# Max-pool, upsample and subtract: the first tile loaded and stored in two pieces of two rows in place of pieces of one, one and two

## The chip, the cores and the metric

The kernel runs on one core of one Trainium2 chip. The metric is the device time of one execution in microseconds, and a kernel's time is the median of several runs.

## The reference

The input x is float32 of shape 8 x 64 x 256 x 256. Every 8 x 8 window of an image is replaced by its maximum, the maxima are repeated back to the full size, and that is subtracted from x:

```python
x_r = x.reshape(B, C, oH, 8, oW, 8)
pooled = x_r.max(axis=(3, 5))
upsampled = np.repeat(np.repeat(pooled, 8, axis=2), 8, axis=3)
return x - upsampled
```

Input and output are 134.22 MB each; every byte is read once and written once.

## The kernel before

Eight image rows (one row of windows) are one "row" of the kernel: 2048 floats, 8 KB, with 32 windows in it. There are 16,384 such rows. A tile gives each of the 128 partitions 4 consecutive rows, 32 KB per partition and 4 MB in all, so there are 32 tiles, numbered 0 to 31. A part of R rows of a tile is R x 8 KB per partition; the profile shows R = 1 as 128x2048 and R = 2 as 128x4096.

The tiles live in SBUF in a ring of 6 slots (`ring`); the window maxima stand in `tops`. Tile i has slot (i - 1) modulo 6, so tile 0 shares slot 5 with tile 6.

Three engines share the work, and semaphores order them:

- SyncE (SP) issues the loads, L110, in order of the tiles. Tile 0 is loaded in pieces, one per entry of `HEAD`, each with a semaphore of its own (`first`); every other tile is loaded in one transfer. From tile 6 on a load first waits until the stores of the tile that had the slot before have landed (`stored`).
- TensorE computes nothing. It waits for the loads' semaphores in order (L117 for the pieces of tile 0, L120 for the others) and adds one to the count `filled` for each.
- VectorE takes one from `filled` (L75), reduces the windows of the part with one max (L81), and subtracts the maxima from the ring in place, one instruction per row (L93). It does that for each piece of tile 0, then in a loop over 5 rounds of 6 slots for tiles 1 to 30, and then for tile 31, which is loaded whole but worked on in the three pieces of `TAIL`, 2, 1 and 1 rows. After the last subtract of a part it adds one to `ready`.
- ScalarE (ACT) computes nothing either. It waits for the count `ready` and issues the store of that part (L129), in the pieces of `HEAD` for tile 0, whole for tiles 1 to 30, in the pieces of `TAIL` for tile 31. At the end it waits for the stores that no later load has waited for.

All loads go through SP's DMA queue, all stores through ACT's, and both queues feed the same 16 DMA engines.

Of the kernel before, what the change touches and what calls it, by code (L numbers as in the profile page):

```python
# [1 line left out]

# [4 lines left out]

F32 = mybir.dt.float32
ROW = 2048


HEAD = [1, 1, 2]
SIZE = 4
ROUNDS = 5
TAIL = [2, 1, 1]
SLOTS = 6


@with_exitstack
def kernel(  # L20
    ctx: ExitStack,
    tc: tile.TileContext,
    x: bass.AP,
    out: bass.AP,
):
    nc = tc.nc
    P = nc.NUM_PARTITIONS
    B, C, H, W = x.shape
    pH = pW = 8
    oW = W // pW  # L30

    x_rows = x.rearrange("b c (oh ph) w -> (b c oh) (ph w)", ph=pH)
    out_rows = out.rearrange("b c (oh ph) w -> (b c oh) (ph w)", ph=pH)
    sizes = [sum(HEAD)] + [SIZE] * (ROUNDS * SLOTS) + [sum(TAIL)]
    assert sum(sizes) * P == x_rows.shape[0] and max(sizes) == SIZE
    starts = [P * sum(sizes[:i]) for i in range(len(sizes))]
    last = len(sizes) - 1

    data = ctx.enter_context(tc.tile_pool(name="data", bufs=1))
    ring = data.tile([P, SLOTS * SIZE * ROW], F32, name="ring")  # L40
    tops = data.tile([P, SLOTS * SIZE * oW], F32, name="tops")
    first = [tc.alloc_semaphore(f"first{i}") for i in range(len(HEAD))]
    loaded = [tc.alloc_semaphore(f"loaded{i}") for i in range(SLOTS)]
    stored = [tc.alloc_semaphore(f"stored{i}") for i in range(SLOTS)]
    final = tc.alloc_semaphore("final")
    filled = tc.alloc_semaphore("filled")
    reduced = tc.alloc_semaphore("reduced")
    ready = tc.alloc_semaphore("ready")

    def slot_of(i):  # L50

        return (i - 1) % SLOTS

    def dram(rows, i):

        n = sizes[i]
        return rows[starts[i] : starts[i] + P * n].rearrange("(p r) d -> p (r d)", r=n)

    def sbuf(i, lo, R):
        at = (slot_of(i) * SIZE + lo) * ROW  # L60
        return ring[:, at : at + R * ROW]

    def top(i, lo, R):
        at = (slot_of(i) * SIZE + lo) * oW
        return tops[:, at : at + R * oW]

    def cuts(parts):
        lo = 0
        for R in parts:
            yield lo, R  # L70
            lo += R

    def take(sem, n):

        nc.vector.wait_ge(sem, n).then_inc(sem, -n)  # L75

    def pool_and_subtract(part, top, R):

        wins = part.rearrange("p (r ph ow pw) -> p r ph ow pw", r=R, ph=pH, ow=oW)
        maxs = top.rearrange("p (r ow) -> p r ow", r=R)  # L80
        nc.vector.tensor_reduce(  # L81
            out=maxs if R > 1 else maxs[:, 0],
            in_=(
                wins.rearrange("p r ph ow pw -> p r ow ph pw")
                if R > 1
                else wins[:, 0].rearrange("p ph ow pw -> p ow ph pw")
            ),
            axis=mybir.AxisListType.XY,
            op=mybir.AluOpType.max,
        ).then_inc(reduced, 1)  # L90
        take(reduced, 1)
        for r in range(R):
            sub = nc.vector.tensor_tensor(  # L93
                out=wins[:, r],
                in0=wins[:, r],
                in1=maxs[:, r].unsqueeze(1).unsqueeze(3).to_broadcast([P, pH, oW, pW]),
                op=mybir.AluOpType.subtract,
            )
        sub.then_inc(ready, 1)

    with tc.tile_critical(no_gpsimd_drain=True):

        landed = [0] * SLOTS
        for i in range(len(sizes)):
            slot = slot_of(i)
            if landed[slot]:
                nc.sync.wait_ge(stored[slot], 16 * landed[slot])
            for k, (lo, R) in enumerate(cuts(HEAD if i == 0 else [sizes[i]])):
                part = slice(lo * ROW, (lo + R) * ROW)
                nc.sync.dma_start(out=sbuf(i, lo, R), in_=dram(x_rows, i)[:, part]).then_inc(  # L110
                    first[k] if i == 0 else loaded[slot], 16
                )
                landed[slot] += 1


        for k in range(len(HEAD)):
            nc.tensor.wait_ge(first[k], 16).then_inc(filled, 1)  # L117
        for i in range(1, len(sizes)):
            turn = (i - 1) // SLOTS + 1
            nc.tensor.wait_ge(loaded[slot_of(i)], 16 * turn).then_inc(filled, 1)  # L120


        done = n_final = 0
        for i in range(len(sizes)):
            for lo, R in cuts(HEAD if i == 0 else TAIL if i == last else [SIZE]):
                part = slice(lo * ROW, (lo + R) * ROW)
                done += 1
                nc.scalar.wait_ge(ready, done)
                nc.scalar.dma_start(out=dram(out_rows, i)[:, part], in_=sbuf(i, lo, R)).then_inc(  # L129
                    stored[slot_of(i)] if i + SLOTS <= last else final, 16  # L130
                )
                n_final += i + SLOTS > last
        nc.scalar.wait_ge(final, 16 * n_final)


        for lo, R in cuts(HEAD):
            take(filled, 1)
            pool_and_subtract(sbuf(0, lo, R), top(0, lo, R), R)
        with nc.vector.Fori(0, ROUNDS):
            with nc.vector.Fori(0, SLOTS) as slot:  # L140
                take(filled, 1)
                pool_and_subtract(
                    ring[:, bass.ds(slot * (SIZE * ROW), SIZE * ROW)],
                    tops[:, bass.ds(slot * (SIZE * oW), SIZE * oW)],
                    SIZE,
                )
        take(filled, 1)
        for lo, R in cuts(TAIL):
            pool_and_subtract(sbuf(last, lo, R), top(last, lo, R), R)


# [1 line left out]
_INS = ['x']  # L153
_OUTS = [((8, 64, 256, 256), 'float32')]


# [23 lines left out]
```

## Time and profile before

| what | before |
|---|---|
| runs | 642.45, 643.52, 644.19 us; median 643.52 |
| profiled execution | 644.19 us, of which the span from the first to the last instruction is 642.4 |
| VectorE busy | 562.8 us, 88% of the span |
| VectorE idle before L81, for the count at L75 | 61.4 us in 27 waits |
| DMA | 268.44 MB, 418 GB/s over the span |
| loads of 4 MB, from issue to landing | 57.2 us (median of 31) |
| stores of 4 MB, from issue to landing | 44.8 us (median of 30) |
| max of one row, two rows, four rows | 2.28, 4.42, 8.69 us |
| subtract of one row | 2.29 us |

Engine names in the profile: DVE is VectorE, ACT is ScalarE, SP is SyncE, POOL is GpSimd; a q behind a name is the engine's instruction queue (SPq, ACTq, DVEq), which is where DMAs are issued and semaphores waited for. In the timeline a line has the start, the time taken (for a DMA line the stretch over which its issues lie), the engine, the line of the kernel, the operation, and in square brackets how long the engine idled before it and what ended that. In the table of windows the columns are the stretch, its length, VectorE's and GpSimd's busy time, the granted clock of TensorE, the share of the time in which the 16 DMA engines were busy, and what they moved in GB/s. The page's row of digits is the same share in 40 slices of 16 us. The trace also has a record of every DMA packet: its queue, its size, its start and its duration.

### The profile page before, as it was taken

The page shows a single profiled execution, that of the slowest core. Times are in us where ns is not written, and L with a number is a line of the kernel's source. Part 1 is how long each engine was busy: PE and PEld are TensorE (multiplying, and loading weights), DVE is VectorE, ACT ScalarE, POOL GpSimd, SP SyncE. Part 2 cuts the span into 40 slices and gives each one's busy share as a digit, 9 for nine tenths or more (in the row PEclk, how much of TensorE's full clock was granted, in tenths as well). Part 3 has the DMA queues.
Part 4 walks back from the last instruction along what each step waited for, and adds up shares of the span by engine and source line. Part 5 has one row for each costly group of instructions (what it writes and reads, how often), then busy time and mean ns, then how long its engine had stood idle before and what let it go on. Part 6 is the DMA issues. An engine that isn't in the chain of part 4 may idle for free. (4 is left out here: it accounts for less than half of the span.)

```text
span 642.4 us, 619 instructions
## 1 busy us (share of the span) xinstructions
DVE 562.8 (88%) x164; POOL 0.2 (0%) x4
## 2 busy tenths in 40 slices
DVE  6999999998889888889888998889988899888991
POOL 0000000000000000000000000000000000000000
DMA  9999999999999999999999999999999999999994
GB/s 367 441 416 441 424 422 433 431 437 422 420 424 437 424 416 431 414 433 424 416 422 420 428 428 414 426 422 426 424 420 424 426 420 426 424 424 412 428 418 203
DMA packets 10080, 268.44 MB, mean 418 GB/s; under 512 B 1120, under 2 KB 1120, under 8 KB 1120
## 3 DMA queue, kind: packets, MB, share of 16 engines
q1 hardware_dynamic: 4896, 134.22, 50.1%
q10 hardware_dynamic: 5184, 134.22, 48.5%
HBM read 134.22 MB, written 134.22 MB: 418 GB/s over the span
## 5 line engine op out<-in xcount | busy, mean ns | idle before, releaser
L81 DVE TENSOR_REDUCE tops<-ring (+2 forms) x36 | 278.5, 7736 | 61.4 <-DVEq L75 61.4
L93 DVE TENSOR_TENSOR ring<-ring,tops (+1 forms) x128 | 285.1, 2286 | 5.3 <-DVEq L75 0.2
L164 POOL MEMSET const-uint8-127<- 128x1 uint8 x1 | 0.1, 102 | 0.0
L164 POOL MEMSET const-bfloat16-1.0<- 128x1 bf16 x1 | 0.1, 101 | 0.0
L164 POOL MEMSET const-float32-0.0<- 128x1 f32 x1 | 0.1, 98 | 0.2 <-issue 0.2
L164 POOL MEMSET const-float32-1.0<- 128x1 f32 x1 | 0.1, 98 | 0.0
## 6 DMA issues: line engine op xcount, KB each, us to landing
ring<-in_x_dram SPq DMA_DIRECT2D x31, 4096.0 KB, 57.2
out_dram<-ring ACTq DMA_DIRECT2D x30, 4096.0 KB, 44.8
out_dram<-ring ACTq DMA_DIRECT2D x4, 1024.0 KB, 13.9
out_dram<-ring ACTq DMA_DIRECT2D x2, 2048.0 KB, 19.6
ring<-in_x_dram SPq DMA_DIRECT2D x2, 1024.0 KB, 5.6
ring<-in_x_dram SPq DMA_DIRECT2D x1, 2048.0 KB, 11.1
```

The source lines that it names most:

```text
L81: nc.vector.tensor_reduce(out=maxs if R > 1 else maxs[:, 0], in_=(wins.rearrange("p r ph ow pw -> p r ow ph pw") if R > 1 else wins[:, 0]. ...
L93: sub = nc.vector.tensor_tensor(out=wins[:, r], in0=wins[:, r], in1=maxs[:, r].unsqueeze(1).unsqueeze(3).to_broadcast([P, pH, oW, pW]), op ...
L164: nc = _bacc.Bacc("TRN2", target_bir_lowering=False, num_devices=1)
```

## The change

One constant changes. Tile 0 is loaded, worked on and stored in two pieces of two rows:

```diff
-HEAD = [1, 1, 2]
+HEAD = [2, 2]
```

In the instructions of the engines this gives: SP issues two loads of 128x4096 in place of two of 128x2048 and one of 128x4096; TensorE waits for two semaphores of tile 0 in place of three; VectorE has one max of 128x4096 in place of two of 128x2048 at the start, with the same four subtracts of one row in tile 0; ACT issues two stores of 128x4096 for tile 0 in place of two of 128x2048 and one of 128x4096. Tiles 1 to 31 are as they were.

## The prediction

> **What bounds the kernel now.** I read the page first, then the timeline at both ends, then the windows of the last 14 us, then the waits of the queue that issues loads. The page:
>
> ```profile
> DVE 562.8 (88%) x164; POOL 0.2 (0%) x4
> ...
> DMA  9999999999999999999999999999999999999994
> GB/s 367 441 416 441 424 422 433 431 437 422 420 424 437 424 416 431 414 433 424 416 422 420 428 428 414 426 422 426 424 420 424 426 420 426 424 424 412 428 418 203
> ```
>
> VectorE has gaps; the 16 DMA engines have none until the last slice. 268.44 MB in 642.4 us is the 418 GB/s of the page, so only three things can move the end: the moment when the DMA engines get work, the time that the packets take, and idle engines before the end.
>
> The timeline at the start shows who waits for whom there:
>
> ```profile
> 0.94 4.01 SPq L110 DMA_DIRECT2D ring<-in_x_dram  x8
> 5.77 2.29 DVE L81 TENSOR_REDUCE tops<-ring 128x32 f32<-128x2048 f32 x1 [5.77 <-DVEq L75]
> ...
> 10.53 32.96 ACTq L129 DMA_DIRECT2D out_dram<-ring  x4
> ...
> 15.05 4.41 DVE L81 TENSOR_REDUCE tops<-ring 128x64 f32<-128x4096 f32 x1
> 19.61 4.49 DVE L93 TENSOR_TENSOR ring<-ring,tops 128x2048 f32<-128x2048 f32 x2
> 25.38 8.69 DVE L81 TENSOR_REDUCE tops<-ring  x1 [1.28 <-DVEq L75]
> ```
>
> SP issues all eight loads that need no free slot (three pieces of tile 0, five whole tiles) within 4 us, so a load is queued from then on whatever VectorE does. The waits of SP's queue say that the later ones come when a store frees a slot:
>
> ```profile
> SPq L110 <- DMA out_dram<-ring: 539.8, 26, 48.6
> ```
>
> Those loads take 57.2 us from issue to landing and the stores 44.8 us (the page's DMA issues), against some 19.7 us for a tile loaded and a tile stored (8.39 MB at about 425 GB/s). So two to three tiles wait in each queue. The trace's packet records say the same: from 3 us to 608 us the 16 engines together idle for 4 us of some 9,700.
>
> At the end:
>
> ```profile
> 611.19 4.42 DVE L81 TENSOR_REDUCE tops<-ring 128x64 f32<-128x4096 f32 x1 [2.31 <-DVEq L75]
> ...
> 627.22 2.29 DVE L93 TENSOR_TENSOR ring<-ring,tops 128x2048 f32<-128x2048 f32 x1
> ```
>
> ```profile
> 632.00:634.00 2.00, 0.00 (x0) 0.00 (x0) 1.00 0.71 299
> 634.00:636.00 2.00, 0.00 (x0) 0.00 (x0) 1.00 0.40 168
> 636.00:638.00 2.00, 0.00 (x0) 0.00 (x0) 1.00 0.22 94
> 638.00:640.00 2.00, 0.00 (x0) 0.00 (x0) 1.00 0.10 41
> 640.00:642.00 2.00, 0.00 (x0) 0.00 (x0) 1.00 0.03 12
> ```
>
> The DMA share (next to last column) falls in steps: most engines are done by 634 to 637 us, and one alone works to 641. By the packet records the last store, issued at 629.5, begins on the idle engines at 630.4 and ends there by 634.1 to 634.7; on the slowest engine it begins only at 638.5, behind a backlog without a gap, and ends at 640.96. So the end is set by the slowest DMA engine's own queue, with 638.5 - 630.4 = 8.1 us to spare against VectorE's last tile.
>
> **The change part by part.** HEAD turns tile 0's pieces of 1, 1 and 2 rows into two pieces of 2 rows.
>
> First landing. TensorE passes the first 1 MB piece on at 5.58 us and the second at 8.04; one 2 MB piece holds the bytes of both, so it comes at 8.04, and VectorE starts at about 8.2 in place of 5.77: 2.4 us later.
>
> VectorE on tile 0. The 2-row piece took 15.05 to 24.13, 9.08 us, and before it the two 1-row pieces took 9.2. Hence the first store is issued at 8.2 + 9.1 = 17.3 (before 10.53) and the second at 26.3 (before, the last piece at 24.13). Two reduces of 2.28 become one of 4.41: 0.15 us less work.
>
> Tile 1. It landed at 25.05. It now meets fewer store packets and lands at about 23.3, while VectorE is free only at 26.3: it starts tile 1 some 0.9 us later than 25.38. Its steady wait disappears there; from about 130 us on it waits for loads again (61.4 us in all at L75 before), so 0.9 us is absorbed.
>
> Arbitration of the two queues. This is the part that moves most. The packet records show load and store packets alternating on each engine, a packet being one partition's piece of a transfer: 8 KB takes 309 ns, 16 KB 611, 32 KB 1213. Tile 0's stores are three of 8 packets per engine, 24 in all, now two of 8, 16 in all, each one paired with a 32 KB load packet. Before: the first store packet ran at 14.83, after 2 load packets of tile 1; 24 pairs later, 26 load packets in, tile 0 was stored (53.96). After: issued 6.8 us later, by when about 7 load packets have run (issue to first packet took 4.3 us); 16 pairs later, 23 packets in. Loads lead stores by 3 packets less from there to the end: 3 x 1.213 = 3.64 us. No engine idles for it, but the last load lands 3.64 us later and VectorE's last tile, 18.4 us of reduce and subtract, moves with it: the last store is issued at 633.1 in place of 629.5.
>
> What covers that: the slowest engine's backlog, 8.1 us before, 8.1 - 3.6 = 4.5 after. The faster engines end near 634.7 + 3.6 = 638.3, still under 641. If that cover were gone, every further microsecond would count in full.
>
> Work of the DMA engines. Bytes are the same. Per engine 32 packets of 8 KB (16 loaded, 16 stored) become 16 of 16 KB; back to back they start 306 and 607 ns apart in the records, so 32 x 306 - 16 x 607 = 80 ns less, and two completion packets of 9 ns go: about 0.1 us gain. One SP issue (0.43 us), one ACT issue and one wait of TensorE on a first semaphore go, all behind queued transfers: nothing. No wait is added.
>
> Two rows and two rules. The second 1 MB piece landed 8.04 - 5.58 = 2.46 us after the first, just its 8 packets at 306 ns, so a transfer less in a queue that is never empty saves nothing beyond its packets. The Trainium skill's DMA: Bandwidth & Descriptors (Anatomy of one DMA) puts about 2 us of fixed cost on each transfer; by that, as an estimate, one load and one store fewer would make the sum 4 us faster. The engines' idle time between 3 and 608 us is nothing, so what started earlier with the small pieces did not end earlier. The skill's Perfetto Trace Analysis (DMA Optimizations) says that splitting transfers lets some start sooner and may end the task sooner where the DMA engines are generally idle, which speaks against undoing a split.
>
> Packet time. What no sum fixes is the slow packets. Load packets take 172 us more than their usual time in total, 10.8 us per engine, and most of that at the first packets of a whole tile. The change shifts where a store begins against a load: from 2 packets after a load tile's first (26 modulo 8) to 1 before the next (23 modulo 8). Bounds: from load 13 to 28, odd tiles lose 9.6 us and even ones 3.9 (sum over 16 engines), a difference of 0.36 us per engine. All 15 even tiles made like the odd: 5.3 us slower; all 16 odd ones made like the even: 5.7 faster. I take zero, because odd and even tiles have the same distance to the store queue in the trace and yet differ by 2.5 times: that distance is not what makes them slow.
>
> Sum: 644.19 us for the profiled execution (642.4 span and 1.8 around it) - 0.1 = 644.1; that execution is 0.7 above the median of the three runs, 643.52, so 643.5 rounded, with the median's own spread of about 1 us.
>
> **The rivals.**
>
> Slow tile starts grow (slower). Place: the first packets of whole loads. Price 0.36 us for each even tile that turns slow, up to 5.3 us, 648.8; it decides from 6 tiles on (2.1 us). For it: load and store boundaries move against each other, and the slow packets cluster there. Against it: the odd-even pattern above. 0.19.
>
> The same effect in the other direction: up to 5.7 us faster, 637.8. Same reasons. 0.17.
>
> VectorE becomes the end (slower). If the slowest engine's backlog did not cover the shift, say because the first store's 6.8 us delay and the 3.6 us both reach the last tile, the end would be 10.4 - 8.1 = 2.3 us later: 645.8. Against it: VectorE waited 2.31 us for the last tile in the profile, so its early delay is lost on the way. 0.05.
>
> **How the numbers follow.** Forecast, 0.59: the DMA engines' queues absorb the change; its own range is 642.0 to 645.0, the spread of runs. About 0.3% (1.9 us) is what a measurement of this kernel can tell from no change. Faster 0.17, same 0.59, slower 0.24, each rival in its class. The range 640.0 to 647.0 takes in the forecast, the small halves of both packet rivals and the VectorE rival, and leaves out about 0.2.
>
> **What would show it.** Right: first reduce near 8.2, two stores of 16 KB packets from 17.3 and 26.3, tile 1's reduce near 26.3 with no wait; SP's first waiting load issued near 50 in place of 53.9; loads about 61 us and stores about 41 us from issue to landing; VectorE's last tile starting near 614.8 with its last subtract near 631; DMA share still in steps to about 641. Wrong: the last store's packets starting on all engines together at the very end (VectorE ends it), idle DMA engines before 600 us, or load packets whose total excess over their usual time moves by more than 30 us over 16 engines.

## The result and the profile after

The changed kernel takes 627.51 us (six runs, 627.13 to 627.91) against 643.57 us of the kernel before (642.45 to 644.19): a ratio of 0.9752, 95% interval 0.974 to 0.9765. The forecast was 643.5 with a range from 640 to 647, so it was wrong: 16 us were gained where none were expected.

The page after, the lines of VectorE's work and of the DMA (profiled execution 627.26 us, span 625.5):

```profile
span 625.5 us, 613 instructions
...
DVE 562.6 (90%) x163; POOL 0.2 (0%) x4
...
GB/s 369 402 434 438 436 434 436 434 436 434 434 432 427 425 434 436 436 436 434 436 434 436 434 434 427 430 425 436 436 436 434 436 436 434 434 436 434 425 427 363
...
DMA packets 9792, 268.44 MB, mean 429 GB/s; under 512 B 1088, under 2 KB 1088, under 8 KB 1088
```

VectorE's work is the same to 0.2 us. What differs is the row of GB/s: 434 to 436 in most slices, where the kernel before has 412 to 441 around 424. The same bytes move faster, from the third slice on.

The start of the timeline is as the forecast worked it out:

```profile
8.47 4.42 DVE L81 TENSOR_REDUCE tops<-ring 128x64 f32<-128x4096 f32 x1 [8.47 <-DVEq L75]
...
17.57 26.96 ACTq L129 DMA_DIRECT2D out_dram<-ring  x3
...
26.42 8.68 DVE L81 TENSOR_REDUCE tops<-ring  x1
```

VectorE starts 2.7 us later than before, the first store is issued 7 us later, tile 1 starts 1 us later and without a wait. Everything at the start is later, and the kernel ends 16.9 us of span earlier. The table of windows shows the end (next to last column: the DMA engines' busy share):

```profile
618.00:620.00 2.00, 0.00 (x0) 0.00 (x0) 1.00 0.87 369
620.00:622.00 2.00, 0.00 (x0) 0.00 (x0) 1.00 1.04 438
622.00:624.00 2.00, 0.00 (x0) 0.00 (x0) 1.00 0.63 266
624.00:626.00 2.00, 0.00 (x0) 0.00 (x0) 1.00 0.00 0
```

The steps of the kernel before, with one engine working alone to 641, are gone: by the packet records the 16 engines now end between 623.2 and 624.0, before between 632.9 and 641.0.

The packet records give the account. Packets took 184 us more than their usual times in the kernel before (309, 611 and 1213 ns for 8, 16 and 32 KB), 11.5 us per engine; after, 23 us, 1.4 per engine, and nearly all of that before 25 us. That is 10.1 us of the 16.9. The slowest engine ended 5.9 us after the mean of the 16 and now ends 0.6 after it: another 5.3. The remaining 1.5 us is idle time of the DMA engines, 1.6 us per engine before (1.4 of it between 608 and 631 us) and nothing after.

### The profile page after: what moved, and what is told of

The parts are those of the page before. It is cut to its first block, busy times and chain, and to the rows that moved or that the text cites. A ratio compares the mean times of both kernels' runs of the same rounds, so it can differ in the third digit from the quotient of the medians.

```text
span 625.5 us, 613 instructions
## 1 busy us (share of the span) xinstructions
DVE 562.6 (90%) x163; POOL 0.2 (0%) x4
## 6 DMA issues: line engine op xcount, KB each, us to landing
ring<-in_x_dram SPq DMA_DIRECT2D x31, 4096.0 KB, 62.1
out_dram<-ring ACTq DMA_DIRECT2D x30, 4096.0 KB, 35.9
```

## The experiments

Two numbers serve for all of them, both read from the packet records. A record does not name its engine; the 16 are told apart by following each one's packets, as the next starts 3 to 4 ns before the one ahead of it ends. The lead is how many 32 KB load packets an engine has begun when tile 1's first store packet begins; the phase is the lead modulo 8, the packets of a tile on one engine. As load and store packets alternate, the lead set in the first 55 us stays as long as both queues have work: 26 in the kernel before and 24 in the changed one, the same at tile 1 and at tile 28. The theories: A, the phase decides; B, the pieces of tile 0 decide by their size and number; C, the distance in tiles between what is read and written decides. The first forecast's model, in which packet times depend on none of it, is the fourth.

| kernel | load packets before the first store | lead | phase | time, us | slow packets' excess after 100 us, loads |
|---|---|---|---|---|---|
| before, [1, 1, 2] | 2 | 26 | 2 | 643.6 | 150 us |
| changed, [2, 2] | 8 (7 on two engines) | 24 (23) | 0 (7) | 627.5 | 0.1 |
| e1_two_two_late | 10 (9 on two engines) | 26 (25) | 2 (1) | 675.6 | 84 (and stores 209 in all) |
| e2_one_three | 2 | 21 (22 on three engines) | 5 (6) | 627.4 | 0.0 |
| e3_two_one_one | 8 (7 on three engines) | 32 (31) | 0 (7) | 627.3 | 0.1 |
| e4_store_waits_two | 6 | 30 | 6 | 627.7 | 0.0 |
| e5_lead25 | 9 (8 on four engines) | 25 (24) | 1 (0) | 627.3 | 0.1 |
| e6_lead27 | 3 | 27 | 3 | 627.4 | 0.2 |
| e7_lead28 | 4 (5 on five engines) | 28 (29) | 4 (5) | 627.5 | 0.1 |
| e8_four_pieces | 2 | 34 | 2 | 642.5 | 153 |
| e9_tiles_permuted | 2 | 26 | 2 | 643.9 | 165 |
| e10_one_two_one | 2 | 26 | 2 | 643.7 | 165 |
| e11_late_lead34 | 10 (9 on four engines) | 34 (33) | 2 (1) | 650.9 | 56 (and stores 103 in all) |
| e12_lead31 | 7 (6 on four engines) | 31 (30) | 7 (6) | 627.8 | 0.0 |

**First group: pieces, phase or distance.** In e1 two extra reduces (results not used) hold VectorE back ahead of tile 0. The helper `hold` adds one reduce for each number in its list, over that many of the 32 windows of a row:

```diff
-HEAD = [1, 1, 2]
+HEAD = [2, 2]
...
+            if lo == 0:
+                hold([32, 4])
```

> HEAD [2, 2] as in the changed kernel, with two extra reduces of tile 0 (2.3 and 0.3 us, result not used) ahead of the first piece, so that the first store comes some 2.6 us, two 32 KB packets, later. Lead means how many 32 KB load packets an engine has begun when tile 1's first store packet begins: 26 in the kernel before, 24 in the changed one. Theory A (the lead's position within a tile, lead modulo 8, decides): lead 26, phase 2 as in the kernel before, and its time, about 643, with load packets losing some 160 us in all. Theory B (the pieces of tile 0 themselves, their sizes and number of transfers, decide): as the changed kernel, about 627.5 to 630.

Measured: 675.6 us, ratio 1.0491 (1.0425 to 1.0557). B falls: the pieces are those of the changed kernel, the first store comes two packets later, and the time is 48 us longer. A holds in sign, but not in size: 675 was expected by nobody. The windows of this run show where its extra time lies:

```profile
600.00:610.00 10.00, 6.37 (x3) 0.00 (x0) 1.00 0.88 377
610.00:620.00 10.00, 9.85 (x3) 0.00 (x0) 1.00 0.44 190
620.00:630.00 10.00, 8.37 (x4) 0.00 (x0) 1.00 0.55 236
630.00:640.00 10.00, 9.85 (x4) 0.00 (x0) 1.00 0.56 239
640.00:650.00 10.00, 8.46 (x3) 0.00 (x0) 1.00 0.67 285
```

Half of the DMA engines' time is idle there. The ends of one tile's load on the 16 engines lie 19 us apart at 245 us and 42 us for the last tile; a tile counts as loaded only when the slowest engine has its part, so the faster engines run out of work. In the kernel before the spread grows to 13 us, in the changed one it stays at 2.0.

In e2 and e3 only the constant differs:

```diff
-HEAD = [1, 1, 2]
+HEAD = [1, 3]        # e2
+HEAD = [2, 1, 1]     # e3
```

> HEAD [1, 3]: the first store as early as in the kernel before (2 load packets in), but only 16 store packets for tile 0, so a lead of 18, phase 2 as before, with loads running two and three tiles ahead of the stores in place of three and four. Theory A (lead modulo 8): slow, about 643. Theory C (the distance in tiles between what is read and written decides, four tiles being slow): fast, about 627. Theory B (fewer or larger pieces are good): fast.

Measured: 627.4 us, ratio 0.9741 (0.9713 to 0.977), but at lead 21, not 18: the second store is issued only after 26 us, the store queue stood empty from 26 to 31, and the loads ran on alone. So this run says nothing against A and is one more phase (5) that is fast.

> HEAD [2, 1, 1]: first store as late as in the changed kernel (8 load packets in), 24 store packets, so a lead of 32, phase 0 as in the changed kernel, with loads four tiles ahead of the stores throughout. Theory A (lead modulo 8): fast, about 627. Theory C (four tiles apart is slow): slow, 643 or far more, as all packets are four tiles apart. Theory B (three pieces are bad): about 643.

Measured: 627.3 us, ratio 0.974 (0.9712 to 0.9769), at lead 32. C falls: loads are four tiles ahead of stores throughout and nothing is slow. So does B's form in which a third piece costs.

In e4 the kernel before keeps its pieces, and only its first store waits for the second piece:

```diff
-                nc.scalar.wait_ge(ready, done)
+                nc.scalar.wait_ge(ready, max(done, 2))
```

> The kernel before, HEAD [1, 1, 2], with one edit: the first store waits until two pieces are ready, so it is issued at about 15.2 us in place of 10.5, some 4 load packets later. Loads, VectorE's work and all transfers are as before. Lead about 30, phase 6. Theory A: the time changes, as the phase does; if only phase 2 is bad, about 627. Theory B (pieces decide): 643.5. The first forecast's model (packet times do not depend on any of it): 643.5.

Measured: 627.65 us, ratio 0.9746 (0.9718 to 0.9774): the whole gain of the change from a wait added to one store. The timeline of this run at the start, and its row of GB/s:

```profile
10.49 2.28 DVE L81 TENSOR_REDUCE tops<-ring 128x32 f32<-128x2048 f32 x1
...
15.23 27.43 ACTq L129 DMA_DIRECT2D out_dram<-ring  x4
```

```profile
GB/s 369 432 423 419 436 436 436 436 436 436 436 436 436 434 419 429 429 434 436 436 436 436 436 436 434 436 434 425 432 429 427 436 436 434 436 436 436 436 436 337
```

VectorE and the loads start as in the kernel before; the first store is issued at 15.23 in place of 10.53, and from the fifth slice on the DMA engines mostly move 436 GB/s.

**Second group: which phases.** e5, e6 and e7 add one extra reduce ahead of the first piece, `hold([16])` (1.2 us) to HEAD [2, 2], and `hold([16])` and `hold([32])` (2.3 us) to HEAD [1, 1, 2]; e8 has HEAD [1, 1, 1, 1].

> HEAD [2, 2] with one extra reduce of half a row (about 1.2 us) ahead of the first piece: the first store one load packet later than in the changed kernel, lead 25, phase 1. If only phase 2 is bad: 627.5. If a store that starts anywhere within the first packets of a load tile is bad (phases 1 to 3): 640 or more.

> The kernel before, HEAD [1, 1, 2], with one extra reduce of half a row (about 1.2 us) ahead of the first piece: the first store one load packet later, lead 27, phase 3. If only phase 2 is bad: 627.5. If phases 1 to 3 are bad: 640 or more. The first forecast's model: 643.5.

> The kernel before with one extra reduce of a whole row (2.3 us) ahead of the first piece: lead 28, phase 4. If only phases near 2 are bad: 627.5. If the time falls off gradually with the distance from phase 2: between 630 and 640. The first forecast's model: 643.5.

Measured: 627.3, 627.4 and 627.45 us, ratios 0.9743 (0.9714 to 0.9771), 0.9745 (0.9716 to 0.9773) and 0.9745 (0.9717 to 0.9774). All fast, one packet on either side of 26 and two above it: the effect does not fall off, it is one place. e6 is the plainest case:

```profile
5.99 1.22 DVE L107 TENSOR_REDUCE spare<-ring 128x16 f32<-128x1024 f32 x1 [5.99 <-DVEq L76]
...
11.87 4.98 ACTq L143 DMA_DIRECT2D out_dram<-ring  x2
```

```profile
GB/s 369 419 419 436 436 436 436 436 436 436 436 436 419 419 436 436 436 436 436 436 436 436 436 434 436 425 417 434 436 436 436 436 436 434 436 436 436 436 432 341
```

This is the kernel before with 1.22 us of useless work on VectorE at its start, and it is 16 us faster.

> HEAD [1, 1, 1, 1]: the first store as early as in the kernel before (2 load packets in), 32 store packets for tile 0, so lead 34: phase 2 again, but one tile more of distance between what is read and what is written. If the phase within a tile decides: slow, 640 to 675. If the lead of 26 packets itself, as a distance in bytes, is what is bad: 627.5.

Measured: 642.5 us, ratio 0.9982 (0.9971 to 0.9993). Lead 34 is slow as 26 is, and 32 is not: the phase counts, not the lead as a distance.

**Third group: checks on the phase.** e9 takes the tiles in another order from DRAM:

```diff
-    starts = [P * sum(sizes[:i]) for i in range(len(sizes))]
+    starts = [P * SIZE * (i * 11 % len(sizes)) for i in range(len(sizes))]
```

> The kernel before, HEAD [1, 1, 2], lead 26, phase 2, with the tiles taken from DRAM in another order (tile i is block 11 i modulo 32 of input and output), so that what is read and what is written at the same time lie other distances apart. If the position of a store's start in a load tile is what costs (transfer boundaries in the queues): as before, about 643. If it is the distance of the addresses: some other time, 627.5 if the distance was the cause.

Measured: 643.9 us, ratio 0.9999 (0.9988 to 1.001). The distance in whole tiles between the DRAM addresses of concurrent loads and stores is not the cause. Each tile's own layout stays as it was, so this run does not exclude a dependence on addresses within a tile, which moves with the phase.

e10 has HEAD [1, 2, 1], e11 HEAD [2, 1, 1] with `hold([32, 4])`, e12 the kernel before with `hold([32, 32, 12])`.

> HEAD [1, 2, 1]: first store as early as in the kernel before and 24 store packets for tile 0, lead 26, phase 2. Phase theory: slow, 643 or above. Theory that the pieces' order matters: other than 643.

> HEAD [2, 1, 1] (627.3 at lead 32) with the same two extra reduces as in the run that took 675: lead 34, phase 2, with a first tile of 2 rows and a late first store. Phase theory: slow. If reaching phase 2 by a late first store is what made 675 out of 643: 660 or more; if that came from the lead of 26 with HEAD [2, 2] alone: 643.

> The kernel before with extra reduces of 2.3, 2.3 and 0.9 us ahead of the first piece: the first store about 4.5 to 5 load packets later, lead 30 or 31, phase 6 or 7, the last phase not yet run. Phase theory with phase 2 alone bad: 627.5.

Measured: 643.65 (ratio 1.0005, 0.9986 to 1.0024), 650.9 (1.0122, 1.0027 to 1.0217) and 627.8 us (0.9762, 0.9728 to 0.9797). With e12 every phase has been run: 2 is slow in six kernels, 0, 1, 3, 4, 5, 6 and 7 are fast in eight (phases 1 and 7 on twelve engines, the other four one phase lower). e11 shows that a late arrival at phase 2 is worse than an early one, as in e1, but with 651 it is nearer to 643 than to 675. In both the engines are further apart when the stores begin: tile 0's first store ends over 1.4 to 1.6 us, 0.35 in the kernel before. That alone is not slow, as it is 1.0 to 1.6 in the changed kernel, e3, e5, e7 and e12. What the two have alone is engines of phases 1 and 2 side by side. By the packet records the engines at phase 1 are the ones that end last: in e11 the four lose 20 to 26 us each in slow store packets, 94 of the 103 us, and in e1 the two lose 45 and 51 us each in stores and at most 1 us in loads after 25 us. In e5 phase 1 stands beside phase 0 and loses at most 0.6. So it is the mixture that goes with the longer times; no run sets it apart from the late start.

**Fourth group: is it the ends of transfers?** The packet records show the order of packets on one engine where a load tile ends; L and S are load and store packets of 32 KB, a star is the 9 ns packet that completes a transfer, and a number is what a packet took beyond its usual time, in ns. First the kernel before (from 264.6 us), then the changed one (from 300.0 us):

```
L S L* S L+963 S* L+119 S
S L S* L S L* S L S L
```

In the kernel before, a load's end and a store's end lie two turns apart with the new load's first packet between them, and this packet or one of the next two is slow, in the odd tiles from 13 to 21 on at least fifteen of the 16 engines within 2 to 7 us. In the changed kernel the store's end comes first. Whether the nearness of the ends makes the packets slow was put to runs whose transfers have other ends. e13, e14 and e15 split every 4-row transfer by partitions, for HEAD [2, 2], [1, 1, 2], and [2, 2] with `hold([16])`:

```diff
+    def halves(R):
+        return [slice(0, 64), slice(64, P)] if R == SIZE else [slice(0, P)]
...
+                for h in halves(R):
+                    nc.sync.dma_start(out=sbuf(i, lo, R)[h], in_=dram(x_rows, i)[h, part]).then_inc(
```

> The changed kernel, HEAD [2, 2], with every load and store of 4 rows split into two transfers of 64 partitions, so that on each engine a transfer is 4 packets and its completion, 5 turns, in place of 8 packets and its completion, 9 turns. Turn theory: the queues take turns, completions included; what costs is that a load's completion and a store's completion lie two turns apart with one load packet of the new transfer between them. The changed kernel's first store follows 8 load turns (here 9, with one completion more) and tile 0's stores are 18 turns: 26 modulo 9 is 8, good; here 27 modulo 5 is 2, the bad place. So slow, 640 or more. If the place within the 8 packets of a tile decides and not the completions, or the pieces decide: about 627.5 to 628.5.

> The kernel before, HEAD [1, 1, 2], with the same split in halves. Before: 2 load turns and 27 store turns, 29 modulo 9 is 2, bad; here 29 modulo 5 is 4, good. Turn theory: 627.5 to 628.5, although the first store comes as early as in the kernel before and there are 60 transfers more each way. If the number or size of transfers costs: 643 or more.

> The split changed kernel with one extra reduce of half a row (1.2 us) ahead of the first piece: 10 load turns and 18 store turns, 28 modulo 5 is 3 (or 29, 4). Turn theory: good, 627.5 to 628.5. If the split itself costs with HEAD [2, 2]: as slow as the split without the extra reduce.

Measured: two runs each, 808 and 827, 818 and 843, 785 and 888 us. These say nothing of the ends, as another limit comes in ahead of it. The page of e13, of its 827 us execution:

```profile
DMA packets 10768, 268.44 MB, mean 325 GB/s; under 512 B 2064, under 2 KB 2064, under 8 KB 2064
...
q1 hardware_dynamic: 5248, 134.22, 57.4%
q10 hardware_dynamic: 5520, 134.22, 41.5%
```

The DMA engines are as busy as ever and move 325 GB/s (343 in the 785 us execution of e15); a load packet of 32 KB takes 1.87 us in the mean against 1.22 in the changed kernel, a store packet 1.33 against 1.21. Inconclusive.

e16, e17 and e18 split by rows instead, all 128 partitions, packets of 16 KB; e17 and e18 add `hold([8])` and `hold([17])`:

```diff
+    def pairs(lo, R):
+        return [(lo, 2), (lo + 2, 2)] if R == SIZE else [(lo, R)]
...
+                for a, n in pairs(lo, R):
+                    part = slice(a * ROW, (a + n) * ROW)
+                    nc.sync.dma_start(out=sbuf(i, a, n), in_=dram(x_rows, i)[:, part]).then_inc(
```

> The changed kernel with every load and store of 4 rows split into two transfers of 2 rows over all 128 partitions: packets of 16 KB, 8 and a completion per transfer. Unlike the split by partitions every engine keeps its 8 partitions, so packets should take their usual 611 ns and the run 627.5 to 630, unless it happens to start a store 2 packets into a load (then 640 or more). The run serves to place the next one: in the transfer theory a store that begins 2 packets into either half of a load tile is slow; in the theory of the place within a tile only one of them is.

> The run with transfers of 2 rows (629.9 us, where tile 1's first store began 41 load packets of 16 KB after tile 0's loads: 1 packet into the second half of a load tile), with one extra reduce of a quarter row (0.6 us, one such packet) ahead of the first piece: lead 42, 2 packets into the second half of a tile. Transfer theory (a store transfer that begins 2 packets into a load transfer is slow, wherever in a tile): slow, 640 or more. Place theory (2 packets, or 64 KB, into a whole tile): fast, 630.

> The same with an extra reduce of half a row and one window (1.2 us, two such packets): lead 43, 3 packets into the second half of a tile. Both theories: fast, 630. If an extra reduce by itself costs with these transfers: as slow as the run with the quarter row.

Measured: 629.9, 630.3 and 630.5 us, ratios 0.9798 (0.9736 to 0.9859), 0.9803 (0.9742 to 0.9864) and 0.9807 (0.9746 to 0.9868), with leads of 41, 42 and 43 packets of 16 KB on most engines. In e17 a store transfer begins 2 packets into a load transfer on ten of the 16 engines (1 on four, 3 on two), and load packets lose 0.3 us in all after 100 us. So the nearness of the ends counted in packets is not enough by itself; but these packets are also half as long, and the store begins in the second half of a tile. Which of the two spares the kernel is open.

What stays open, then, is the mechanism: that a store transfer beginning two 32 KB packets into a load transfer goes with slow packets is shown by fourteen kernels, why it does is not. The ends of transfers, and addresses within a tile, remain as causes that no run tells apart.

## Why the prediction was wrong

The steps that were read from rows held. The first reduce came at 8.47 (forecast 8.2), the first store at 17.57 (17.3), tile 1's reduce at 26.42 without a wait (26.3); loads take 62.1 us from issue to landing (61). The lead fell by 2 packets where 3 were forecast: fourteen of the 16 engines had begun 8 load packets by the first store, not 7. Late starts cost nothing, as the DMA queues were never empty, and the end stayed with the DMA engines: the last store was issued at about 616.2 us and its first packet began at 620.7. VectorE's last tile began at 597.89, not at 614.8, as everything behind the loads moved with them; the stores' 35.9 us (41 forecast) belongs to the same gain. The rows after:

```profile
597.89 4.42 DVE L81 TENSOR_REDUCE tops<-ring 128x64 f32<-128x4096 f32 x1 [1.50 <-DVEq L75]
...
ring<-in_x_dram SPq DMA_DIRECT2D x31, 4096.0 KB, 62.1
out_dram<-ring ACTq DMA_DIRECT2D x30, 4096.0 KB, 35.9
```

One reading was off and changed nothing: in the kernel before, the seven engines that begin the last store at 630.4 end at 632.9 to 633.0, not at 634.1 to 634.7. The slowest engine's 640.96, from which the sum goes, was read rightly.

The step that failed is the one on packet time, a term put at zero. The measured term is the load packets' excess, which fell from 172 to 23 us over the 16 engines, far beyond the 30 us that the prediction itself named as a sign of being wrong. The reason for the zero was that odd and even tiles "have the same distance to the store queue in the trace and yet differ by 2.5 times: that distance is not what makes them slow". That does not follow. A condition that holds for all tiles can't be seen by comparing tiles with each other; the odd-even difference comes on top of it, and why odd tiles lose more stays open. e4 to e8 show the distance to be the condition.

The bound was wrong for the same reason: the gain was priced by turning odd tiles into even ones, 5.7 us at most. The nearest row for a kernel without slow packets was in the same trace: loads 2 and 4 lost 0.2 and 0.0 us over all engines. With it the term is the whole excess of 10.8 us per engine, and the slowest engine's further distance from the mean, 5.9 us, hangs on the same packets: a bound near 17 us (10.8 + 5.9), where 16 was measured. The rival of slow tile starts that shrink had the mechanism and the direction, at 0.17 and with a third of the size. Its counterpart was no fancy either: a phase that is worse exists (e1, 675 us), but this change did not go there.

The two rules weighed there: the fixed cost per transfer of the Trainium skill (DMA: Bandwidth & Descriptors, Anatomy of one DMA), which that section gives for transfers issued by GpSimd, did not show for these, issued by SP and ACT: e3 and e4 with one load and one store more are as fast as the changed kernel. The skill's rule on splitting transfers is for DMA engines that are generally idle (Perfetto Trace Analysis, DMA Optimizations). These were not (4 us of some 9,700 between 3 and 608 us), and more pieces were no gain by themselves: [2, 1, 1] takes 627.3 us as [2, 2] does. That the pieces would set a phase for 600 us, no row said.

## What to carry to other kernels

Where two DMA queues alternate without ever running empty, as here, their relative position is set once at the start and kept (24 or 26 packets from tile 1 to tile 28); so an edit at the start can change the rate of the whole run. When a kernel is bound by DMA and its packets have two classes of duration, take the fast class as the bound for what an edit may gain, and try a few positions of the first store, by a wait or a delay of one packet each: here that is worth 16 us of 643, and one more microsecond of work on VectorE gets it. Look at the spread of the DMA engines' ends too: a load is done when its slowest engine is.

## What the runs showed of the hardware

- Load and store queue take turns packet by packet, and a packet here is one partition's piece of a transfer, up to 32 KB; so 8 KB store pieces beside 32 KB load pieces get a fifth of the bytes, and tile 0's two 1 MB stores in the kernel before took 15.7 and 23.2 us from issue to their last packet.
- Steady reading and writing together reached 436 GB/s in slices of 16 us, without slow packets for over 500 us.
- At one phase of eight, 642 to 676 us in place of 627: in the kernel before, a load packet takes up to 1.3 us longer at the start of a load, in some tiles on every engine, and in the six slow kernels the engines' ends of the last load lie 11 to 42 us apart. Where engines of phase 1 ran beside engines of phase 2 (e1, e11), those of phase 1 had slow store packets and ended last.
- Transfers of 64 partitions (2 MB, packets of 32 KB) moved 319 to 343 GB/s with the DMA engines busy (e13 to e15); transfers of the same size over 128 partitions (16 KB packets) moved 427 (e16 to e18).
